# Attention: one unit in eight transposed on TensorE instead of by DMA

## The chip, the cores and the metric

One core of one Trainium2 chip runs the kernel. The metric is the device time of one execution in microseconds (us).

## The reference

Two layers of a backbone over 1024 latent tokens with 256 context tokens in front, width 1024. A layer projects the normed tokens once, into three parallel mixers (softmax attention, an mLSTM, a pooling mixer), joins them, projects them out, adds them to the stream, and applies a SwiGLU feed-forward. The change touches the attention alone:

```python
def one_block(qi):                      # 128 queries, 8 heads of 64, 2 key/value heads
    s = jnp.einsum('bqhgd,bkhd->bhgqk', qi, k, preferred_element_type=F32) * scale
    p = jax.nn.softmax(s, -1).astype(v.dtype)
    return jnp.einsum('bhgqk,bkhd->bqhgd', p, v)
```

Latent queries read all 1280 keys; context queries (layer 0 alone needs them) read the 256 context keys.

## The kernel before

Precision comes from pairs: an fp32 value is held as an f16 high part and an f16 remainder, and a product is three f16 matmuls (`TERMS`).

The attention stage of a layer begins at `phase("s")`. Its work is a list of units: one head of one tile of 128 latent queries (64 a layer), and in layer 0 also four units that hold four heads of a tile of context queries. Step i of the loop does these, in this order of the program:

- `front` of unit i: the scores, six matmuls into `Sp`, 128 x 1280 in PSUM (two such buffers); VectorE takes the row maximum `mx`; ScalarE writes the exponentials to `pf`, fp32 in SBUF (two buffers), with the row sums on the side.
- `split` of unit i-1: `pf` is cast to f16 (on ScalarE; on VectorE where the unit's index is divisible by 8) and GpSimd subtracts, which gives the pair `phl` (three buffers). One DMA transpose from SyncE's queue turns the pair into `pT` (five buffers), with the keys on the partitions.
- a fill: now and then one product of the output projection (`wout`, 12 f16 matmuls into `pwo`, which VectorE adds into the residual X). `pace` gives each step a budget, and a product of n columns costs n / 200 of it. Its weights are loaded by SyncE's queue (`st`) and split by ScalarE and VectorE (`hl`).
- `back` of unit i-5: 30 matmuls with `pT` as weights, into `pv`. After the eighth head `att_finish` scales the tile and turns it with another DMA transpose (`aoh`).
- one step of background threads (`pump`), the norms of finished token blocks among them.

In this stage PSUM holds two score buffers of three banks (`bank3`) and two single banks (`bank`). `pv` keeps one single bank for the eight heads of its tile; `pwo` and the norms take the other.

The Tile framework puts each engine's instructions in order by priority and readiness, close to the program's order, and places the semaphores; a buffer is reused when its last reader is done. Helpers record their operations at their own lines: L152 is `act` (ScalarE), L166 `stt` (VectorE), L169 `tt` (VectorE or GpSimd).

Of the kernel before, what the change touches and what calls it, by code (L numbers as in the profile page):

```python
# [10 lines left out]
F16 = mybir.dt.float16  # L11
# [7 lines left out]
P = 128  # L19
# [62 lines left out]
def hybrid_kernel(ctx: ExitStack, tc: tile.TileContext, I, out, dbg=None):  # L82
    nc = tc.nc
    V, S, G, TE, DMA = nc.vector, nc.scalar, nc.gpsimd, nc.tensor, nc.sync
    MUL, ADD, SUB, MAX, MIN = ALU.mult, ALU.add, ALU.subtract, ALU.max, ALU.min
# [10 lines left out]
    PFB, PHB, PTB = 2, 3, 5  # L96
# [21 lines left out]
    def bank(name="bk"):  # L118
        return cur["b"].tile([P, 512], F32, tag="bk", name=name)
# [8 lines left out]
    def pt_(shape, dt, tag, bufs=1, name=None):  # L128
        return cur["w"].tile(list(shape), dt, tag=tag, name=name or tag, bufs=bufs)
# [9 lines left out]
    def after(i, j):  # L139
        tc.add_manual_dep(i, j.name, order, reason="table order")  # L140

    def preload():

        p = S.preload_act_table_set("natural_log_exp_and_others").ins
        for j in tabs["last"]:
            after(p, j)
        tabs.update(pre=p, last=[], kind="el")

    def act(o, i, f=AF.Copy, **kw):
        if f in (AF.Exp, AF.Ln) and tabs["kind"] != "el":  # L150
            preload()
        b = S.activation(o, i, f, **kw).ins  # L152
        if f in (AF.Exp, AF.Ln):
            after(b, tabs["pre"])
            tabs["last"] = tabs["last"][-7:] + [b]
        elif f in (AF.Tanh, AF.Silu):
            if tabs["kind"] != f:
                for j in tabs["last"]:
                    after(b, j)
                tabs.update(last=[], kind=f)  # L160
            for j in tabs["last"][-1:]:
                after(b, j)
            tabs["last"] = [b]
# [4 lines left out]
    def tt(o, a, b, op, e=None):  # L168
        (e or V).tensor_tensor(o, a, b, op=op)  # L169
# [23 lines left out]
    def pump(n=1):  # L193
        for _ in range(n):
            for g in list(threads):
                try:
                    next(g)
                except StopIteration:
                    threads.remove(g)
# [18 lines left out]
    idn = con.tile([P, P], F32, name="idn")  # L218
# [305 lines left out]
    class Sums:  # L524


        def __init__(self, t0, n):
            self.t0, self.n, self.acc, self.k = t0, n, [], 0
# [212 lines left out]
    for l in range(DEPTH):  # L741
# [554 lines left out]

        class Unit:
            def __init__(self, i, qt, hs, qs):
                self.i, self.qt, self.hs, self.qs = i, qt, hs, qs
                self.nk, self.k0 = (NTOK, 0) if qt < 8 else (TC, T)  # L1300
                self.n = self.nk * len(hs)

# [25 lines left out]
                        accum_out=self.qs[1][:, h:h + 1])  # L1328

            def split(self):  # L1330
                i, n, pf = self.i, self.n, self.pf
                hl = pt_((P, 2, NTOK), F16, "phl", PHB)
                if i % 8 == 0:
                    V.tensor_copy(hl[:, 0, :n], pf[:, :n])
                else:
                    act(hl[:, 0, :n], pf[:, :n])
                tt(hl[:, 1, :n], pf[:, :n], hl[:, 0, :n], SUB, G)
                self.pT = pt_((P, 2, 10, P), F16, "pT", PTB)
                if n == NTOK:
                    DMA.dma_start_transpose(out=self.pT.rearrange("p a k c -> p (a k) c"), in_=hl.rearrange("p a t -> p (a t)"))  # L1340
                else:
                    for a in range(2):
                        DMA.dma_start_transpose(out=self.pT[:, a, :n // P], in_=hl[:, a, :n])

            def back(self):
                if self.hs[0] == 0:
                    self.qs[0] = bank("pv")
                nkt = self.nk // P
                for e, h in enumerate(self.hs):
                    kv = h // 4  # L1350
                    for kt in range(nkt):
                        for j, (a, b) in enumerate(TERMS):
                            mm(self.qs[0][:, h * 64:h * 64 + 64], self.pT[:, a, e * nkt + kt],
                               qkv[:, 6, b, self.k0 + kt * P:self.k0 + (kt + 1) * P][:, kv * 64:kv * 64 + 64],
                               start=(kt == 0 and j == 0), stop=(kt == nkt - 1 and j == 2))

        def att_finish(qt, pv_, sums):
            V.reciprocal(sums, sums)
            o = f2k((P, 8, 64), F32, "ao")
            tt(o, pv_.rearrange("p (h e) -> p h e", h=8), sums.unsqueeze(2).to_broadcast([P, 8, 64]), MUL)  # L1360
            oh = f2k((P, 4, 2, P), F16, "aoh")
            ov = o.rearrange("p (k x) e -> p k (x e)", x=2)
            act(oh[:, :, 0], ov)
            tt(oh[:, :, 1], ov, oh[:, :, 0], SUB)
            DMA.dma_start_transpose(out=mixT[:, 0:4, :, qt * P:(qt + 1) * P].rearrange("p k a t -> p (k a) t"),
                                    in_=oh.rearrange("p k a c -> p (k a c)"))
# [9 lines left out]
        def fills():  # L1376
            ctx_ = [] if last else [(T, TC)]
            sums = {}
            for key, k0, bl, qt in (("woa", 4, blks, -1), ("wob", 0, ctx_ + [(0, 512)], 3), ("woc", 0, [(512, 256)], 5)):
                if k0 == 0:  # L1380
                    for t0, n in bl:
                        sums[t0] = Sums(t0, n)
                for m in range(8):
                    while done[0] < qt:
                        yield 0
                    w = w_get((key, l, m))
                    for (t0, n) in bl:
                        if k0 == 0 and m:
                            sums[t0].step(G)
                        wout(w, k0, m, t0, n, bank("pwo")[:, :n])  # L1390
                        yield n / 200
                w = None
                if k0 == 0:
                    for t0, n in bl:
                        nt[t0] = chain(norm(l, 3, h2, t0, n, sums[t0].step(V)))
                        del sums[t0]
                if key == "wob":
                    dump(f"mix{l}", mixT)

        def first_ffn():  # L1400

            while now[0] < nu or any(g in threads for g in nt.values()):
                yield 0
            f0.update(wg=w_get(("gate", l, 0)), wu=w_get(("up", l, 0)), Sg=bank3("Sg"), Su=bank3("Su"))
            for t0, n in blks[2:] + [(0, 512)]:
                for w, S_ in ((f0["wg"], f0["Sg"]), (f0["wu"], f0["Su"])):
                    yield from fm_steps(S_[:, t0:t0 + n], w, h2, t0, n)
# [10 lines left out]
        units = []  # L1418
        for qt in range(8):
            qs = [None, pt_((P, 8), F32, "sums", 3)]  # L1420
            units += [Unit(len(units) + h, qt, [h], qs) for h in range(8)]
            if qt < 2 and not last:
                qs = [None, pt_((P, 8), F32, "sums", 3)]
# [2 lines left out]
        nt = {}  # L1426
        fill = fills()
        nu = len(units)
        budget = 0.0
        fill_ffn = first_ffn()  # L1430

        def pace(part):

            return (1.1 if part < 0.9 else 2.5) if last else 0.8 if part < 0.2 else 1.5

        for i in range(nu + 5):
            now[0] = i
            if i < nu:
                units[i].front()
            if 1 <= i <= nu:  # L1440
                units[i - 1].split()
            if i >= 3:
                budget = min(budget + pace(i / nu), 3.0)
                if budget > 0:
                    c = next(fill, None)
                    if c is None:
                        c = next(fill_ffn, 0)
                    budget -= c
            if i >= 5:
                u = units[i - 5]  # L1450
                u.back()
                if u.hs[-1] == 7:
                    att_finish(u.qt, *u.qs)
                    if u.qt < 8:
                        done[0] = u.qt
                units[i - 5] = u = None
            pump()
        for _ in fill:
            pass
        units = fill = None  # L1460
# [544 lines left out]
```

## Time and profile before

| | |
|---|---|
| median of three runs | 2797.26 us (2795.92 to 2797.89) |
| the profiled execution | 2801.78 us, span 2800.0 us, mean granted TensorE clock 0.967 |
| busy over the span | TensorE 92%, VectorE 67%, ScalarE 50%, GpSimd 46% |
| attention of layer 0 | scores from 372.6 us, transposes of the pairs from 383.1 us to about 668 |
| attention of layer 1 | scores from 1826.1 us, transposes from 1834.4 us to 2101.1 |

The profile is one execution on the chip. Times in it count from the start of its span. PE is TensorE's matmuls and PEld its weight loads, DVE is VectorE, ACT ScalarE, POOL GpSimd; SPq is SyncE, which issues the DMAs. L12 is line 12 of the kernel.

### The profile page before, as it was taken

The numbers are of one execution on the slowest core, as the hardware profiler recorded it, in microseconds if no ns is written. First come the engines' busy times: TensorE is split into PE (matmuls) and PEld (weight loads), VectorE is DVE, ScalarE is ACT, GpSimd is POOL, SyncE is SP. The second block draws the span as 40 slices with busy tenths as digits, with TensorE's granted clock in tenths as the row PEclk, the third lists the DMA queues.
The fourth block names the chain that finished last, engine by engine and source line by source line (L and its number), as shares of the span: only waits on it lengthen the run. The fifth ranks groups of instructions, "written<-read, shape, count | busy, mean of one in ns | idle before, by whom it ended". The sixth has DMA issues, their size and how long they took to land. (4 is left out here: it accounts for less than half of the span.)

```text
span 2800.0 us, 53595 instructions
## 1 busy us (share of the span) xinstructions
PE 2562.9 (92%) x21331; PEld 1496.8 (53%) x21331; DVE 1883.6 (67%) x3217; ACT 1387.2 (50%) x2650; POOL 1288.5 (46%) x979
## 2 busy tenths in 40 slices
PE   7999988887799999999999998988878799999997
PEld 5875555555455555555555674545554344444444
DVE  5458867779856655656566557866677766576666
ACT  5345457776443434434344445466764444444353
POOL 1124446674434434344443213456764555555651
PEclk9999999999899999999999999999999999999999
DMA  9544499996222232322212222499993121211211
GB/s 298 143 122 115 126 208 187 195 186 129 61 83 84 83 88 80 89 84 83 68 39 78 69 61 64 124 183 188 195 188 80 45 61 53 61 53 53 61 53 76
DMA packets 650640, 300.95 MB, mean 107 GB/s; under 512 B 381896, under 2 KB 639764, under 8 KB 649876
## 3 DMA queue, kind: packets, MB, share of 16 engines
q1 hardware_dynamic: 650212, 297.45, 44.2%
q8 instruction: 167, 2.74, 0.4%
q14 instruction: 85, 0.70, 0.1%
q10 hardware_dynamic: 176, 0.07, 0.0%
HBM read 176.19 MB, written 20.87 MB: 70 GB/s over the span
## 5 line engine op out<-in xcount | busy, mean ns | idle before, releaser
L1900 PEld LDWEIGHTS <-hlp 128*128 128x128 f16 x5040 | 492.9, 98 | 610.1 <-issue 49.5
L1900 PE MATMUL Swb<-T,hlp 128*128 128x512 f16 x1920 | 446.4, 382 | 30.8 <-DVE sg L166 14.7
L169 POOL TENSOR_TENSOR phl<-pf,phl 128x1280 f16<-128x1280 f32 (+1 forms) x132 | 346.3, 2625 | 187.7 <-ACT phl L152 129.4
L166 DVE SCALAR_TENSOR_TENSOR hlp<-ws,hlp 128x512 f16<-128x512 f32 (+1 forms) x320 | 228.9, 722 | 150.6 <-ACT hlp L152 119.9
L152 ACT ACTIVATE hlp<-ws 128x512 f16<-128x512 f32 (+1 forms) x320 | 163.6, 518 | 220.1 <-PE Swb L1900 89.8
L152 ACT ACTIVATE pf<-Sp,mx,rq 128x1280 f32<-128x1280 f32 (+1 forms) x144 | 189.2, 1315 | 103.4 <-DVE mx L1320 89.1
L1315 DVE TENSOR_REDUCE mx<-Sp 128x1 f32<-128x1280 f32 (+1 forms) x132 | 194.9, 1477 | 64.5 <-PE Sp L1311 59.5
L1371 PE MATMUL pwo<-T,hl 128*128 128x512 f16 (+1 forms) x960 | 196.5, 356 | 38.0 <-DVE X L166 20.0
L1900 PE MATMUL Swc<-T,hlp 128*128 128x512 f16 x960 | 227.2, 379 | 0.0
L1311 PE MATMUL Sp<-T 128*128 128x512 f16 (+1 forms) x800 | 172.9, 355 | 58.5 <-ACT pf L152 56.1
L1900 PE MATMUL Swb<-tq,hlp 128*128 128x512 f16 x960 | 220.5, 379 | 2.5 <-ACT T L152 2.3
L466 PE MATMUL pfm<-T,hl 128*128 128x512 f16 (+1 forms) x1032 | 217.0, 364 | 4.2 <-ACT E L152 4.1
L152 ACT ACTIVATE T<-sg 128x512 f16<-128x512 f32 (+1 forms) x170 | 100.0, 600 | 229.4 <-POOL sg L169 154.8
L166 DVE SCALAR_TENSOR_TENSOR hlp<-st,hlp 128x256 f16<-128x256 f32 (+1 forms) x201 | 141.6, 709 | 89.8 <-ACT hlp L152 75.1
L169 POOL TENSOR_TENSOR ws<-st 128x256 f32<-128x256 f32 (+1 forms) x97 | 102.2, 1061 | 185.6 <-DMA st<-in_w_ffn_down_dram 83.3
L1912 PE MATMUL dx<-T,hlp 128*128 128x256 f16 x1440 | 177.9, 273 | 10.6 <-DVE hlp L166 6.4
L169 POOL TENSOR_TENSOR X<-X,T 128x512 f32<-128x512 f32 x80 | 113.2, 1415 | 147.4 <-DVE X L166 111.1
L1900 PE MATMUL Swa<-T,hlp 128*128 128x512 f16 x720 | 169.1, 380 | 0.0
L1912 PEld LDWEIGHTS <-hlp 128*128 128x128 f16 x1440 | 139.3, 100 | 43.0 <-issue 9.1
L1371 PEld LDWEIGHTS <-hl 128*128 128x128 f16 x960 | 98.0, 103 | 119.8 <-issue 53.3
L152 ACT ACTIVATE phl<-pf 128x1280 f16<-128x1280 f32 (+1 forms) x115 | 144.9, 1261 | 30.3 <-DMA pT<-phl 27.9
L152 ACT ACTIVATE hlp<-st 128x256 f16<-128x256 f32 (+1 forms) x201 | 101.2, 510 | 114.6 <-PE Swb L1900 73.2
(320 smaller groups left out, 4733.6 us busy)
## 6 DMA issues: line engine op xcount, KB each, us to landing
T<-in_w_ada_dram SPq DMA_DIRECT2D x48, 512.0 KB
rawa<-in_w_ada_dram SPq DMA_DIRECT2D x48, 512.0 KB
st<-in_w_in_dram SPq DMA_DIRECT2D x32, 512.0 KB
st<-in_w_out_dram SPq DMA_DIRECT2D x64, 256.0 KB
st<-in_w_ffn_gate_dram SPq DMA_DIRECT2D x32, 512.0 KB
st<-in_w_ffn_up_dram SPq DMA_DIRECT2D x30, 512.0 KB
st<-in_w_ffn_down_dram SPq DMA_DIRECT2D x30, 512.0 KB
xs<-X SPq DMA_DIRECT2D x4, 2048.0 KB
```

Source lines behind the costliest of these rows:

```text
L152: b = S.activation(o, i, f, **kw).ins
L166: V.scalar_tensor_tensor(o, a, s, b, op0=o0, op1=o1)
L169: (e or V).tensor_tensor(o, a, b, op=op)
L466: mm(o, w[:, a, k, :], h[:, k, b, t0:t0 + n], start=(k == 0 and j == 0), stop=(k == nk - 1 and j == 2))
L1311: mm(Sp[:, e * nk + b0:e * nk + b0 + m], ql, qkv[:, 4 + h // 4, a, k0 + b0:k0 + b0 + m], start=(a == 0), stop=(a == 1), skip_group_check=True)
L1315: r = V.tensor_reduce(mx[:, :ne], Sp[:, :n].rearrange("p (e k) -> p e k", e=ne), axis=AX.X, op=MAX)
L1371: mm(pb, w[:, a, k, :], mixT[:, k0 + k, b, t0:t0 + n], start=(k == 0 and j == 0), stop=(k == 3 and j == 2))
L1900: mm(o, w[:, a, k, :], B[:, b], start=(s in "172" and k == 0 and j == 0), stop=(k == kh(i) - 1 and j == 2), skip_group_check=True)
L1912: mm(dbank[i][:, r * 256:(r + 1) * 256], w[:, a, k, :], B[:, b], start=(first and k == 0 and j == 0), stop=(not first and k == kh(i) - 1 a ...
```

## The change

Every eighth of the single-head units, from the sixth on, is turned on TensorE: 16 units in all. Such a unit has no `phl`, no DMA transpose and no GpSimd subtraction. Its `pf` is transposed in ten fp32 blocks of 128 x 128, four, four and two to a part. Each part takes one bank, `turn`; ScalarE copies the bank to the high half of `pT`, and VectorE writes the remainder. The three parts are placed in the step of the unit's `split`: before the fill, after the fill, and after `back`.

```diff
             def split(self):
                 i, n, pf = self.i, self.n, self.pf
+                if i in turned:
+                    self.pT = pt_((P, 2, 10, P), F16, "pT", PTB)
+                    self.parts = [self.turn(k, min(4, 10 - k)) for k in range(0, 10, 4)]
+                    return
                 hl = pt_((P, 2, NTOK), F16, "phl", PHB)
...
+            def turn(self, k, m):
+                def go():
+                    tb = bank("turn")
+                    for c in range(m):
+                        TE.transpose(tb[:, c * P:(c + 1) * P], self.pf[:, (k + c) * P:(k + c + 1) * P], idn)
+                    tv = tb[:, :m * P].rearrange("p (k c) -> p k c", k=m)
+                    act(self.pT[:, 0, k:k + m], tv)
+                    tt(self.pT[:, 1, k:k + m], tv, self.pT[:, 0, k:k + m], SUB)
+                return go
...
+        turned = [u.i for u in units if len(u.hs) == 1][5::8]
...
             if 1 <= i <= nu:
                 units[i - 1].split()
+                parts = units[i - 1].parts
+            if parts:
+                parts.pop(0)()
             if i >= 3:
                 budget = min(budget + pace(i / nu), 3.0)
...
+            if parts:
+                parts.pop(0)()
             if i >= 5:
                 u = units[i - 5]
                 u.back()
...
+            while parts:
+                parts.pop(0)()
             pump()
```

## Rows read from the trace of the kernel before

**Rows 1.** The page: busy us by engine, DMA share in 40 slices.

```profile
PE 2562.9 (92%) x21331; PEld 1496.8 (53%) x21331; DVE 1883.6 (67%) x3217; ACT 1387.2 (50%) x2650; POOL 1288.5 (46%) x979
...
DMA  9544499996222232322212222499993121211211
```

**Rows 2.** Stretches: length; busy us of PE, PEld, DVE, ACT, POOL; clock; DMA share; GB/s.

```profile
383.00:605.00 222.00, 195.31 (x2354) 125.62 (x2354) 160.22 (x192) 158.77 (x216) 153.48 (x65) 0.95 1.09 194
605.00:668.00 63.00, 48.68 (x634) 36.29 (x633) 55.97 (x68) 43.26 (x67) 40.61 (x23) 0.92 0.97 184
1840.00:2080.00 240.00, 194.51 (x2353) 122.22 (x2352) 163.90 (x194) 169.61 (x212) 164.07 (x66) 0.94 1.05 190
2080.00:2105.00 25.00, 18.80 (x308) 15.34 (x306) 22.77 (x27) 17.89 (x28) 15.57 (x10) 0.89 0.91 170
```

**Rows 3.** DMA view, 1840 to 2080 us: DMAs issued, with their count.

```profile
st<-in_w_out_dram SPq DMA_DIRECT2D x18, 256.0 KB
pT<-phl SPq DMA_TRANSPOSE x60
```

**Rows 4.** Timeline of SyncE, 1944 to 1981 us: start, us, issue, count.

```profile
1949.84 13.44 SPq L1340 DMA_TRANSPOSE pT<-phl  x4
...
1964.07 10.85 SPq L1340 DMA_TRANSPOSE pT<-phl  x3
1974.98 1.30 SPq L1365 DMA_TRANSPOSE T<-aoh  x1
```

**Rows 5.** Waits, 1847 to 2058 us: who for whom, us, times, longest.

```profile
ACT pf L152 <- DVE mx L1320: 34.6, 16, 6.1
...
ACT phl L152 <- DMA pT<-phl: 16.1, 11, 3.2
...
DVE phl L1334 <- DMA pT<-phl: 8.0, 3, 3.9
...
POOL phl L169 <- DMA pT<-phl: 3.7, 1, 3.7
```

**Rows 6.** Timeline of ScalarE, 1944 to 1955 us: first and last of four exponentials.

```profile
1944.04 1.42 ACT L152 ACTIVATE pf<-Sp,mx,rq 128x1280 f32<-128x1280 f32 x1 [3.01 <-DVE mx L1320]
...
1952.38 1.42 ACT L152 ACTIVATE pf<-Sp,mx,rq 128x1280 f32<-128x1280 f32 x1
```

**Rows 7.** Timeline of TensorE, 1938 to 1960 us: scores, then a fill.

```profile
1951.18 1.24 PE L1311 MATMUL Sp<-T 128*128 128x512 f16 x6
1952.26 2.75 PE L1371 MATMUL pwo<-T,hl 128*128 128x512 f16 x12
```

**Rows 8.** Groups by line and form, 1840 to 2080 us: busy, mean ns, idle before.

```profile
L169 POOL TENSOR_TENSOR phl<-pf,phl 128x1280 f16<-128x1280 f32 x59 | 155.1, 2629 | 71.8 <-ACT phl L152 55.5 <-DVE phl L1334 9.7 <-DMA pT<-phl 3.7
L1315 DVE TENSOR_REDUCE mx<-Sp 128x1 f32<-128x1280 f32 x59 | 87.6, 1484 | 27.9 <-PE Sp L1311 24.3 <-ACT phl L152 3.5
...
L152 ACT ACTIVATE phl<-pf 128x1280 f16<-128x1280 f32 x52 | 65.8, 1267 | 16.9 <-DMA pT<-phl 16.1
...
L166 DVE SCALAR_TENSOR_TENSOR X<-pwo,prm,X 128x512 f32<-128x512 f32 x23 | 17.2, 746 | 8.2 <-PE pwo L1371 8.2
```

**Rows 9.** Groups by line and form, 383 to 605 us.

```profile
L169 POOL TENSOR_TENSOR phl<-pf,phl 128x1280 f16<-128x1280 f32 x52 | 137.4, 2643 | 61.9 <-ACT phl L152 51.7 <-DVE phl L1334 7.4 <-POOL phl L169 1.2
```

**Rows 10.** Timeline of TensorE, 5 to 60 us: eight fp32 transposes each.

```profile
23.17 1.95 PE L233 MATMUL px<-idn,T 128*128 128x128 f32 x8
...
50.23 1.04 PE L233 MATMUL px<-idn,T 128*128 128x128 f32 x8
```

**Rows 11.** Instructions on `ptm`, a PSUM bank: count, ns min/median/max.

```profile
L152 ACT ACTIVATE T<-ptm x6: 383/578/597, 366.3 to 1825.2; 128x512 f16<-128x512 f32 x4, 128x256 f16<-128x256 f32 x2
L166 DVE SCALAR_TENSOR_TENSOR T<-ptm,T x6: 425/684/692, 367.4 to 1825.6; 128x512 f16<-128x512 f32 x4, 128x256 f16<-128x256 f32 x2
```

**Rows 12.** Stretches of the start, columns as in rows 2.

```profile
20.00:30.00 10.00, 5.99 (x57) 4.10 (x57) 4.92 (x8) 3.38 (x7) 0.00 (x0) 0.50 1.09 343
...
50.00:57.00 7.00, 6.77 (x71) 4.57 (x69) 4.80 (x10) 5.52 (x14) 2.21 (x2) 1.00 1.08 368
```

More of the change, by code (lines that the diff above doesn't have):

```diff
@@ L1298, in __init__ @@
             def __init__(self, i, qt, hs, qs):
-                self.i, self.qt, self.hs, self.qs = i, qt, hs, qs
+                self.i, self.qt, self.hs, self.qs, self.parts = i, qt, hs, qs, []
                 self.nk, self.k0 = (NTOK, 0) if qt < 8 else (TC, T)
@@ L1439, in hybrid_kernel @@
                 units[i].front()
+            parts = []
             if 1 <= i <= nu:
                 units[i - 1].split()
+                parts = units[i - 1].parts
+            if parts:
+                parts.pop(0)()
             if i >= 3:
```

## The prediction

> **What bounds the kernel now.** I read the page first, for where the time is spent: its slices show two stretches in which the DMA engines are at nine tenths or more, slices 6 to 9 and 26 to 29 [rows 1]. They are the two attention stages. The reader is to see there that TensorE, at 92% over the span, is not what stands out in them; the DMA engines are.
>
> Next, the view by stretches for those stages [rows 2]. In 383 to 605 us and 1840 to 2080 us the DMA share is 1.09 and 1.05 (packets overlap, so it passes 1), while TensorE is busy 195 of 222 and 195 of 240 us, ScalarE 159 and 170, VectorE 160 and 164, GpSimd 153 and 164. In the tails, 605 to 668 and 2080 to 2105, VectorE leads with 56.0 of 63 and 22.8 of 25.
>
> The DMA view counts 60 transposes `pT<-phl` in the 240 us [rows 3], so a unit takes 4.00 us. SyncE's own timeline says why: four transposes in 13.44 us and three in 10.85, with nothing between [rows 4], 24.3 / 7 = 3.47 us each. Eight units cost the queue 8 x 3.47 = 27.8, plus one transpose of `aoh`, 1.3, plus the `w_out` loads (18 in 60 units, so 2.4, at the 0.79 us between the end of the four transposes and the next three) 1.9: 31.0 of the 32.0 us that eight units take. So the queue is 97% occupied, and the waits show its pressure going back: ScalarE 16.1, VectorE 8.0 and GpSimd 3.7 us until a `phl` buffer was free [rows 5]. The larger wait for the row maximum, 34.6, follows from it in part, since VectorE is blocked behind its own cast. When nothing holds it, ScalarE starts four exponentials in a row between 1944.04 and 1952.38, 2.78 us apart [rows 6]. The front end can run faster than 4.00.
>
> The stretch moves 190 GB/s while the DMA engines never rest [rows 2]. The Trainium skill (Advanced Engine Details and Errata, X-Bar Transpose) expects 350 to 400 GB/s of a transposing DMA; as an estimate from that page, a unit's 128 x 2560 x 2 bytes would take 1.9 us at 350, the queue would stand half empty, and relieving it would be worth nothing. The trace disagrees with 3.47 us, and the measurement decides.
>
> **The change part by part.** It concerns 16 units of 132, eight in a layer: 5, 15, 25, 33, 41, 49, 57, 65 in layer 0 and 5, 13, ..., 61 in layer 1.
>
> *Removed*, per turned unit: one DMA transpose, 3.47 us of the queue; one GpSimd subtraction, 2.63; one ScalarE cast, 1.27 [rows 8] (none of the 16 has an index divisible by 8, where VectorE casts).
>
> *Added*: ten fp32 transposes of 128 x 128. The start of the program has the same instruction: eight take 1.04 us [rows 10], so 0.13 each and, with what the last of a group takes to end, about 0.6 for four and 0.38 for two, 1.6 for a unit. ScalarE copies out of PSUM to f16: 0.60 for 512 columns, 0.38 for 256 [rows 11], 1.58 in all, against 1.27 removed. VectorE subtracts out of PSUM: 0.68 and 0.42, 1.8 us in all, all of it new.
>
> *Eight units after*, layer 1: the queue 31.0 - 3.5 = 27.5; TensorE 194.5 / 60 x 8 = 25.9, plus 1.6 = 27.5. Both floors stand at 27.5, so the slack against 32.0 is 4.5. In layer 0's stretch GpSimd has 52 long units [rows 9] and the four context units, 56 in 222 us, 31.7 for eight; TensorE 195.3 / 56 x 8 = 27.9, plus 1.6 = 29.5, is the floor there: slack 2.2. ScalarE's 0.3 more and VectorE's 1.8 cost nothing in these stretches, where both are idle for a quarter of the time or more; in the tails VectorE's is priced. GpSimd's 2.63 less gains nothing by itself, as it is idle for a third.
>
> *The new wait.* One of the two banks of `bank()` is held by `pv` through a q tile, so the three parts and the fills (`pwo`) take turns in the other. And `pf` has two buffers: the exponential two units later waits until the last transpose has read it. Before, `pf` is free 1.27 + 2.63, with hand-overs some 4.1 us after its exponential. After, bare: 0.6 + 0.60 + 0.68, twice, plus 0.38: 4.2. Behind each of the two copies and subtractions that come first something can stand: half an exponential (0.7) on ScalarE and half a maximum (0.75) on VectorE, 2.9 for two. So `pf` is held h = 0.1 to 3.0 us longer. If a fill comes in between as well, its 2.75 [rows 7] and 0.75 for the add into X [rows 8] make it 6.5. I take 1.6: halfway between the first two, because TensorE starts a fill right behind the scores, at 1952.26 after the scores of 1951.18 [rows 7], while an exponential starts at 1952.38 [rows 6]; such a fill is ahead of the transposes, not between them. What queues behind a late `pf` is the exponential two units on, and behind that its scores buffer.
>
> *The sum.* Layer 1, seven units in the stretch: -(4.5 - 1.6) x 7 = -20.3. Layer 0, six: -(2.2 - 1.6) x 6 = -3.6. Three units (57 and 65, and 61 of layer 1) fall into the tails, where no queue is relieved: hold 1.6 plus VectorE's 1.8 at 90% occupation, 1.6: 3 x 3.2 = +9.6. Together -14.3; as a function of the hold, 16 h - 39.9. The profiled execution took 2801.8 us (span 2800.0); it would take 2787.5. It stands 4.5 above the median of the runs, 2797.3; the same step down from the median gives 2783. With h = 0.1 layer 1 gains no more than the queue's 3.5: -24.5 - 12.6 + 5.1 = -32, or 2765.
>
> **The rivals.** *The single bank decides (slower).* A fill gets between the first and the second part. The budgets of `pace` (0.8 a step, then 1.5, in layer 0, 1.1 in layer 1, against 2.56 for 512 columns), followed through the loop, put a fill into the very step of 11 of the 16 units: eight of 512 columns (3.5 us of bank each, as above) and three of 256 (about half, 1.9). That adds 8 x 3.5 + 3 x 1.9 = 33.7, and -14.3 becomes +19: 2817. It decides as soon as the mean hold passes 39.9 / 16 = 2.5 us. For it: the program puts the fill between the two parts. Against it: a fill's inputs are ready earlier than the transposes'. The Trainium skill speaks on this side (Perfetto Trace Analysis, Optimizing Tensor Performance): independent groups should rotate through different banks, so that evacuating one overlaps the next. No stretch shown here has transposes in one bank; what the rule would do here is this rival.
>
> *The queue is not the bound (no change).* SyncE would issue the transposes earlier and another loop keep the 4.00 us. For it: direct waits on the DMA are only 16.1 + 8.0 + 3.7 = 27.8 of 211 us, and a chain of waits among the three engines could set the same pace. Against it: the 97%. Time: 2797, give or take 5. The DMA rule above would lead here, and the row leaves it little.
>
> *TensorE's clock falls (slower).* Waits for the bank are gaps on TensorE. Eight transposes took 1.95 us where the granted clock was 0.50, 1.04 at 1.00 [rows 10, 12]; the stages stand at 0.94 and 0.95, the last tail at 0.89 [rows 2]. If both stages fell to 0.89, TensorE's eight units would take 25.9 x 0.94 / 0.89 + 1.6 = 29.0 and 27.9 x 0.95 / 0.89 + 1.6 = 31.4, the slacks would be 3.0 and 0.3, and the sum -(3.0 - 1.6) x 7 + (1.6 - 0.3) x 6 + 9.6 = +7.6: 2805.
>
> **How the numbers follow.** What a measurement can tell from no change is 0.2%, 5.6 us: h below 2.1 is faster, above 2.9 slower. The forecast, 2783 with 2765 to 2791 of its own, gets 0.47; no change 0.19; the bank 0.30; the clock 0.04. So faster 0.47, same 0.19, slower 0.34. The range, 2764 to 2816, takes in the bare hold and nearly all of the bank's price; it leaves out the full price of a fill between the parts of every unit that has one.
>
> **What would show it.** In the changed profile: 112 long transposes `pT<-phl`, 160 fp32 transposes into `turn`, GpSimd 116 subtractions; layer 1's stage about 17 us shorter (-20.3 + 3.2) and layer 0's some 3 longer (-3.6 + 6.4); the waits of ScalarE, VectorE and GpSimd for a `phl` buffer well below 27.8 in layer 1's stretch; SyncE idle for a few us after each turned unit. The step on the hold is wrong if the last transpose of a turned unit starts much more than 6 us after its exponential ends. The forecast is wrong if fills stand on TensorE between the parts of most units, or if VectorE's subtractions stand behind two maxima, not half of one.

## The result and the profile after

The changed kernel takes 2847.06 us (median of four runs, 2846.34 to 2848.71), the kernel before 2797.57 (four runs, 2795.92 to 2798.91): a ratio of 1.018, with a 95% interval of 1.016 to 1.020, so some 49.5 us slower. The prediction said 2783, at most 2816. The profiled execution has a span of 2845.7 us against 2800.0.

From the first scores to the last `pv`, layer 0's stage grew from 296.4 us (373.8 to 670.2) to 326.9 (375.0 to 701.9), layer 1's from 279.5 (1826.1 to 2105.6) to 291.7 (1857.0 to 2148.8). That is 30.5 + 12.3 of the 45.7 us between the spans.

The page after, busy time by engine and the DMA share in 40 slices, against [rows 1]:

```profile
PE 2591.2 (91%) x21491; PEld 1519.1 (53%) x21491; DVE 1910.4 (67%) x3265; ACT 1392.1 (49%) x2682; POOL 1238.3 (44%) x963
...
DMA  9544488876223222222212222488973111111211
```

Stretches after, columns as in [rows 2]: the body and the tail of layer 0's stage, the body of layer 1's.

```profile
383.00:630.00 247.00, 209.89 (x2428) 137.27 (x2427) 170.66 (x213) 160.79 (x228) 139.30 (x60) 0.94 0.85 159
630.00:690.00 60.00, 45.19 (x559) 32.79 (x560) 46.56 (x62) 38.54 (x62) 28.48 (x17) 0.89 0.74 143
1850.00:2110.00 260.00, 212.04 (x2512) 134.91 (x2510) 175.46 (x223) 169.65 (x220) 145.65 (x59) 0.95 0.86 163
```

The queue was relieved: the DMA share in the stages fell from 1.09 and 1.05 to 0.85 and 0.86. The time did not follow. No engine took its place: TensorE is busy 82% of layer 1's stretch (212.0 of 260), VectorE 67%, ScalarE 65%, where they stood at 81, 68 and 71% before. The clock stood at 0.95 and 0.94 before, at 0.94 and 0.95 after. So the stages are longer by waits. The waits after, 1879 to 2094 us (as [rows 5]: who for whom, us, times, longest):

```profile
POOL phl L169 <- ACT phl L152: 56.6, 21, 5.7
...
ACT pf L152 <- POOL phl L169: 21.2, 11, 2.8
PEld L1368 <- DMA pT<-phl: 21.1, 10, 3.4
PE pv L1368 <- DMA pT<-phl: 18.8, 10, 3.3
...
DVE X L166 <- PE pwo L1386: 10.0, 12, 2.0
...
ACT pT L152 <- PE turn L1354: 8.0, 6, 5.6
...
PE turn L1354 <- ACT pf L152: 4.9, 4, 2.5
...
ACT phl L152 <- DMA pT<-phl: 4.7, 4, 2.7
```

Two of these rows in the view before, 1847 to 2058 us:

```profile
POOL phl L169 <- ACT phl L152: 46.6, 33, 3.7
...
ACT pf L152 <- POOL phl L169: 0.5, 1, 0.5
```

The wait that the change was to shorten shrank: ScalarE for a free `phl`, 16.1 to 4.7; the rows of VectorE and GpSimd for one are gone. In its place the exponential waits for the subtraction that frees `pf` (0.5 to 21.2), GpSimd waits longer for the casts (46.6 to 56.6), and `pv` waits for DMA transposes that are issued late behind them. The queue is no longer full; it is fed late.

The matmuls, copies and subtractions on `turn` over the execution, and what TensorE, ScalarE and VectorE waited for ahead of them:

```profile
L1354 PE MATMUL turn<-idn,pf x160: 272/273/476, 400.5 to 2132.9; 128*128 128x128 f32 x160
L152 ACT ACTIVATE pT<-turn x48: 372/586/599, 402.8 to 2135.9; 128x512 f16<-128x512 f32 x32, 128x256 f16<-128x256 f32 x16
L169 DVE TENSOR_TENSOR pT<-turn,pT x48: 407/680/693, 403.7 to 2136.8; 128x512 f16<-128x512 f32 x32, 128x256 f16<-128x256 f32 x16
its engine sat idle before it (us, times) until:
  ACT pf L152: 44.4, 20
  PE turn L1354: 20.1, 17
  ACT pT L152: 14.6, 13
  DVE pT L169: 11.5, 17
```

The durations of the copies and subtractions are those of [rows 11]; four transposes take 0.66 us in the median, though six of the 32 groups take 1.1. The waits are the news: 44.4 us for an exponential (21.3 of TensorE's matmuls and 23.1 of its weight loads, which wait side by side), 20.1 of ScalarE for transposes.

One turned unit of layer 1 (index 13) shows how. TensorE, then ScalarE, VectorE and GpSimd (start, us, instruction, count, idle before it and what ended that):

```profile
1916.09 1.11 PE L1354 MATMUL turn<-idn,pf 128*128 128x128 f32 x4
...
1921.32 2.76 PE L1386 MATMUL pwo<-T,hl 128*128 128x512 f16 x12 [0.20 <-DVE pT L169]
...
1925.76 0.66 PE L1354 MATMUL turn<-idn,pf 128*128 128x128 f32 x4 [0.48 <-DVE X L166]
...
1930.10 0.44 PE L1354 MATMUL turn<-idn,pf 128*128 128x128 f32 x2 [2.40 <-DVE pT L169]
```

```profile
1914.54 1.40 ACT L152 ACTIVATE pf<-Sp,mx,rq 128x1280 f32<-128x1280 f32 x1
...
1917.42 1.42 ACT L152 ACTIVATE pf<-Sp,mx,rq 128x1280 f32<-128x1280 f32 x1 [1.38 <-POOL phl L169]
...
1918.83 0.59 ACT L152 ACTIVATE pT<-turn 128x512 f16<-128x512 f32 x1
...
1923.35 1.42 ACT L152 ACTIVATE pf<-Sp,mx,rq 128x1280 f32<-128x1280 f32 x1 [2.77 <-POOL phl L169]
...
1928.93 1.42 ACT L152 ACTIVATE pf<-Sp,mx,rq 128x1280 f32<-128x1280 f32 x1 [1.77 <-POOL phl L169]
```

```profile
1919.17 1.49 DVE L1315 TENSOR_REDUCE mx<-Sp 128x1 f32<-128x1280 f32 x1 [5.40 <-PE Sp L1311]
1920.58 0.68 DVE L169 TENSOR_TENSOR pT<-turn,pT 128x512 f16<-128x512 f32 x1
...
1926.71 2.74 DVE L166 SCALAR_TENSOR_TENSOR hl<-st,hl 128x512 f16<-128x512 f32 x1 [1.00 <-ACT hl L152]
1929.37 0.68 DVE L169 TENSOR_TENSOR pT<-turn,pT 128x512 f16<-128x512 f32 x1
```

```profile
1926.29 2.61 POOL L169 TENSOR_TENSOR phl<-pf,phl 128x1280 f16<-128x1280 f32 x1 [2.98 <-DVE X L166]
```

The first part starts at 1916.09, right behind its exponential. Its copy comes behind the next exponential, its subtraction behind a row maximum; then the fill takes the bank (1921.32), and the second part starts at 1925.76. Its subtraction stands behind a weight split that takes 2.74 us, and TensorE stands 2.40 us for it. The last part ends at 1930.54, so `pf` is held 14.6 us. Meanwhile one `pf` buffer is left, and the exponentials come 5.9 and 5.6 us apart instead of 2.78 [rows 6]. Over the sixteen units, from the exponential's end to the last transpose's, the mean is 10.6 us (5.9 to 16.1). Before, the same sixteen units held `pf` 4.7 us on the mean (exponential's end to subtraction's end), so the hold grew by 5.9. A fill stands between the first and second part in 11.

### The profile page after: what moved, and what is told of

It is laid out like the page before. It is cut to its first block, busy times and chain, and to the rows that moved or that the text cites. A ratio compares the mean times of both kernels' runs of the same rounds, so it can differ in the third digit from the quotient of the medians.

```text
span 2845.7 us, 53938 instructions
## 1 busy us (share of the span) xinstructions
PE 2591.2 (91%) x21491; PEld 1519.1 (53%) x21491; DVE 1910.4 (67%) x3265; ACT 1392.1 (49%) x2682; POOL 1238.3 (44%) x963
## 5 line engine op out<-in xcount | busy, mean ns | idle before, releaser
L1924 PE MATMUL Swb<-T,hlp 128*128 128x512 f16 x1920 | 444.6, 381 | 30.1 <-ACT T L152 27.3
L169 POOL TENSOR_TENSOR phl<-pf,phl 128x1280 f16<-128x1280 f32 (+1 forms) x116 | 303.3, 2618 | 267.5 <-ACT phl L152 155.2
L1386 PE MATMUL pwo<-T,hl 128*128 128x512 f16 (+1 forms) x960 | 191.2, 350 | 26.1 <-DVE X L166 12.2
L1311 PE MATMUL Sp<-T 128*128 128x512 f16 (+1 forms) x800 | 181.7, 362 | 24.8 <-ACT pf L152 22.5
L1368 PE MATMUL pv<-T,pT 128*128 128x64 f16 x3936 | 150.0, 196 | 32.1 <-DMA pT<-phl 24.7
L1368 PEld LDWEIGHTS <-pT 128*128 128x128 f16 x3936 | 143.3, 100 | 55.4 <-DMA pT<-phl 28.2
```

Source lines behind the costliest of these rows:

```text
L1311: mm(Sp[:, e * nk + b0:e * nk + b0 + m], ql, qkv[:, 4 + h // 4, a, k0 + b0:k0 + b0 + m], start=(a == 0), stop=(a == 1), skip_group_check=True)
L1386: mm(pb, w[:, a, k, :], mixT[:, k0 + k, b, t0:t0 + n], start=(k == 0 and j == 0), stop=(k == 3 and j == 2))
L1924: mm(o, w[:, a, k, :], B[:, b], start=(s in "172" and k == 0 and j == 0), stop=(k == kh(i) - 1 and j == 2), skip_group_check=True)
```

## The experiments

Each was run beside the kernel before on the same chip (2801.2 to 2802.3 us there). Differences are of medians; brackets hold the ratio's 95% interval. "Own buffer" means that a turned unit's exponentials go to `spare`, SBUF that is free in this stage, so that both `pf` buffers stay with the others.

**e1, own buffer; e2, all parts ahead of the fill; e3, both.**

```diff
-                self.pf = pt_((P, NTOK), F32, "pf", PFB)
+                self.pf = spare if self.i in turned else pt_((P, NTOK), F32, "pf", PFB)
```
```diff
-            if parts:
+            while parts:
                 parts.pop(0)()
             if i >= 3:
```

> The changed kernel, but a turned unit writes its exponentials to a place of its own, so that the two buffers of pf serve the other units alone. Theory H (the loss comes from pf, which a turned unit holds 10.6 us after its exponential on the mean, against some 4 before): the loss of 49 us goes, 2780 to 2805 us. Theory B (the loss comes from TensorE, which stands before parts and fills until the one free bank is emptied): nothing but the place has changed, 2835 to 2850.

> The changed kernel, but all three parts stand ahead of the fill of their step. H: the hold falls by the fill's 3.5 us and more, to 5 to 7 us, and most of the loss goes: 2795 to 2820. B: the bank has the same users and only their order differs; fills now wait for three parts: 2835 to 2855.

> Both edits together. H: as the first alone, since a pf of its own makes the order of the parts indifferent, within 8 us of it. B: as the second alone.

Measured: e1 +32.7 us [1.011, 1.014], e2 +52.2 [1.017, 1.020], e3 +42.1 [1.014, 1.017]. So the hold of `pf` is worth 17 us (49.5 - 32.7), not nearly all. e2 takes every fill out from between the parts and shortens the mean hold to 8.5 us, and gains nothing: the three parts then stand on TensorE one behind the other, each until the bank is cleared (its rows ahead of `turn`: DVE pT 18.9 against 11.5 in the change, PE turn 32.1 against 20.1). e3 lies between the two, as neither theory said.

**e4, relief only.** The sixteen units take a constant for their weights: no transposition of theirs at all, no cast, no subtraction, and their `pv` waits for nothing.

```diff
-                    self.pT = pt_((P, 2, 10, P), F16, "pT", PTB)
-                    self.parts = [self.turn(k, min(4, 10 - k)) for k in range(0, 10, 4)]
+                    self.pT = fixed
```

> Leaves out the turning of the 16 units: their weights are a constant, so neither DMA nor TensorE turns anything, and cast and subtraction go too. It shows what the relief of the queue is worth with no price. If the queue set the pace, 13 units at 2 to 3.5 us: 2750 to 2775. If it did not: 2790 to 2800.

Measured: -26.5 us [0.989, 0.992]; layer 0's stage 285.8 us (-10.6), layer 1's 262.4 (-17.0). That is what all the relief is worth together, so what was put in its place costs 76. It isn't the queue's alone: GpSimd's subtraction (2.63 us) and ScalarE's cast (1.27) go with the DMA transpose. e16 below puts work of 1.6 us back on ScalarE and loses nothing by the medians, so the cast is hardly it; no run parts the queue from GpSimd.

**e5, own buffer and the parts one step later; e6, own buffer and one part a step, in the steps u+2 to u+4, behind `back`.**

```diff
                 units[i - 1].split()
-                parts = units[i - 1].parts
+            if 2 <= i <= nu + 1:
+                parts = units[i - 2].parts
```

> The turned unit keeps its own exponential buffer, and its three parts are issued one step later than in e1, so that no transpose stands on TensorE ahead of its exponential. Theory 'order' (TensorE runs its instructions in a fixed order; the first transpose stands in front of pv products and scores until its exponential has ended, about 24 us over both stages, and what is behind it is late): at least 15 us under e1's +33, that is +5 to +18 us against the kernel before, and the waits of turn for an exponential under 5 us. Theory 'bank' (copies and subtractions must clear the one single bank that fills and parts share): +25 to +40, as e1. Theory 'work' (the copies and subtractions cost ScalarE and VectorE their time wherever they stand): +25 to +35.

> As e5, but one part a step, in the three steps that follow the one after the unit's exponential, each behind the step's pv products. Theory 'order': as e5 or better, 0 to +15 us against the kernel before. Theory 'bank': better than e1, since a part has a whole step for its bank, +10 to +20, but with the waits of turn and pwo for the bank gone. Theory 'work': +25 to +35, as e1.

Measured: e5 +9.1 us [1.002, 1.004], e6 +2.0 [1.000, 1.002]. Only the place differs from e1, and most of the 32.7 us is gone. The waits of `turn` for an exponential are gone too. Both keep waits for the bank (rows ahead of `turn`: DVE pT 25.7 and DVE X 9.9 in e5, DVE X 24.8 and DVE pT 9.1 in e6).

**e7, no transposes; e8, no copies**, both with the own buffer and the places of e1.

```diff
-                    tb = bank("turn")
...
-                    tv = tb[:, :m * P].rearrange("p (k c) -> p k c", k=m)
+                    tv = self.pf[:, k * P:(k + m) * P].rearrange("p (k c) -> p k c", k=m)
```

> Leaves out the 160 transposes and the bank: the unit keeps its own exponential buffer, ScalarE copies the same three pieces of it straight into the halves of the weights and VectorE subtracts, so that the sixteen units' weights are not turned. Theory 'work': +15 to +35 us against the kernel before, near e1's +33. Theories 'order' and 'bank': -25 to -10, near e4's -26, since neither TensorE nor a bank takes part.

> Leaves out the copies and subtractions: the unit keeps its own exponential buffer and is transposed on TensorE into the bank as in e1, but nothing reads the bank, and the sixteen units' pv products take other values for weights. Theory 'order': the stall of the first transpose stays, 0 to +20 us against the kernel before. Theory 'bank': -25 to -10, since a part frees its bank as soon as it has ended. Theory 'work': -25 to -10 as well.

Measured: e7 -8.1 us [0.995, 0.998], between the theories; e8 +5.0 [1.001, 1.003]. With nothing reading the bank, the transposes alone take back the relief and more.

**e11, one transpose in place of ten; e12, the same one step later.** Nothing else of the turn is left in them.

```diff
-                    self.parts = [self.turn(k, min(4, 10 - k)) for k in range(0, 10, 4)]
+                    self.parts = [self.turn(0, 1)]
```

> e8 with one transpose instead of ten in each of the sixteen units, at the place of the first part; copies, subtractions and the other nine transposes are left out, and the sixteen units' pv products take other values for weights. The one transpose costs TensorE 0.3 us at most. Theory 'order' (it is the place in front of pv products and scores that costs, by the wait for the exponential): -5 to +10 us against the kernel before, 15 us or more above e4's -26. If e8's +31 over e4 was the transposes' own time: -26 to -20.

> e11 with the one transpose placed one step later. Theory 'order': -26 to -18 us against the kernel before, 15 us or more under e11. Otherwise as e11.

Measured: e11 -2.5 us [0.998, 1.000], e12 -23.3 [0.991, 0.994]. Instructions on `turn` and the waits ahead of them (matmuls and weight loads together), e11 and then e12:

```profile
L1354 PE MATMUL turn<-idn,T x16: 272/328/477, 399.8 to 2080.0; 128*128 128x128 f32 x16
its engine sat idle before it (us, times) until:
  ACT T L152: 54.4, 23
```

```profile
L1354 PE MATMUL turn<-idn,T x16: 272/273/421, 399.4 to 2069.0; 128*128 128x128 f32 x16
its engine sat idle before it (us, times) until:
  DVE X L166: 10.6, 6
```

Sixteen transposes, 16 x 0.3 = 5 us of work, cost 21 us by their place alone: behind the scores of the next unit and ahead of other products, waiting for an exponential that is not done. TensorE's matmuls alone stand 26.0 us for it in e11, in 11 waits; one step later no such wait is left. One of them, on TensorE in e11 (`T` in the second line is the unit's own buffer):

```profile
1941.38 0.55 PE L1365 MATMUL pv<-T,pT 128*128 128x64 f16 x13 [0.34 <-DMA pT<-phl]
1945.62 0.48 PE L1354 MATMUL turn<-idn,T 128*128 128x128 f32 x1 [3.69 <-ACT T L152]
1945.89 0.63 PE L1311 MATMUL Sp<-T 128*128 128x512 f16 x1
1946.32 3.77 PE L1383 MATMUL pwo<-T,hl 128*128 128x512 f16 x12
...
1950.80 0.66 PE L1365 MATMUL pv<-T,pT 128*128 128x64 f16 x17
```

One transpose stands 3.69 us in the middle of a unit's `pv` products, of which 13 are done. Scores, a whole fill and the other 17, which read the same `pT`, follow it, none with a wait of its own. The 21 us are good to about 5: the two profiled executions differ by 17.2, of which 12.8 lie in the two stages.

**e13, e7 with the copies and subtractions one step later; e16, e7 without the subtractions** (the low halves are other values). e13's edit is that of e5; e16 leaves out the `tt` of `turn`.

> e7 (no transposes on TensorE, no bank; ScalarE copies and VectorE subtracts straight from the unit's own exponential buffer, so that the sixteen units' weights are not turned) with the three parts one step later. Theory 'order' (copies and subtractions stand on ScalarE and VectorE in front of other units' work until their input is there): -26 to -18 us against the kernel before, 10 us or more under e7's -8. Theory 'work' (the 1.6 and 1.8 us of the engines are worth what they take, wherever they stand): -12 to -3, as e7.

> e7 without the subtractions: in the sixteen units ScalarE copies the exponentials straight to the weights' high halves in three pieces, the low halves are other values, and there are no transposes and no bank. If ScalarE's copies cost nothing in their place (the engine is idle for a quarter of the time): -28 to -22 us against the kernel before, as e4, and e7's 18 us were the subtractions' and their meeting with GpSimd. If the copies cost their 1.58 us a unit: about -10, as e7.

Measured: e13 +8.8 us [1.002, 1.005], which both theories missed; e16 -26.1 [0.990, 0.993], as e4. So the work of ScalarE's copies costs nothing that the medians show, to within some 6 us (their waits for transposes are not in e16), and e7's 18 us come with the subtractions. VectorE's subtractions in e13:

```profile
L169 DVE TENSOR_TENSOR pT<-T,pT x48: 409/678/2741, 404.0 to 2098.5; 128x512 f16<-128x512 f32 x32, 128x256 f16<-128x256 f32 x16
```

Read from SBUF, some are four times as long as the 0.69 us that none of the 48 passes from PSUM in the change: 13 are over 1 us in e13, 3 in e7 (counted in the instructions' own times), and all 48 take 43.8 us together against 32.6. So VectorE works 11 us more in e13; whether that is what makes it 17 us slower than e7 is not shown. Neither run prices the change's own subtractions.

**e14, e1 with copies and subtractions that read the exponentials in SBUF**, so that the same transposes stand in the same places but a bank is free once they end.

```diff
-                    tv = tb[:, :m * P].rearrange("p (k c) -> p k c", k=m)
+                    tv = self.pf[:, k * P:(k + m) * P].rearrange("p (k c) -> p k c", k=m)
```

> e1 with the copies and subtractions reading the exponentials in SBUF instead of the bank: the same transposes, copies and subtractions in the same places, but nothing reads the bank, and the sixteen units' weights are not turned. Theory 'chain through the bank': +15 to +24 us against the kernel before, 9 us or more under e1's +33. If the parts simply do not add up (the same waits counted otherwise): +28 to +35, as e1.

Measured: +13.2 us [1.004, 1.007], 19.5 under e1, a little below the range of the chain's theory. That is the chain through the single bank: a part, its copy, its subtraction, a fill, its add, the next part. The edit undoes two of its links at once, the copy's wait for the transposes and the bank's wait for copy and subtraction. e14's subtractions are longer than e1's (37.1 us against 28.5 in all), so the chain is not overrated by them. The adds of the fills in layer 0's stage, 374 to 700 us, e1 and then e14 (busy, mean ns, idle before):

```profile
L166 DVE SCALAR_TENSOR_TENSOR X<-pwo,prm,X 128x512 f32<-128x512 f32 x24 | 18.0, 749 | 39.1 <-PE pwo L1386 39.1
```

```profile
L166 DVE SCALAR_TENSOR_TENSOR X<-pwo,prm,X 128x512 f32<-128x512 f32 x24 | 17.9, 746 | 16.9 <-PE pwo L1386 16.9
```

VectorE stands less than half as long for fills once they need not wait for the parts' bank. The gain is in this stage: layer 0's takes 307.0 us in e14 against 321.3 in e1. Layer 1's takes 281.7 against 281.9, though the same wait falls there from 16.6 to 8.8; in layer 1 the chain cost nothing that these executions show.

**e9, e6 in layer 1 alone; e10, e9 with no fill in the four steps of a turned unit; e15 and e17, every fourth unit of layer 1** (in e15 the third part reads what the next turned unit has written to the shared buffer; in e17 it comes a step earlier).

```diff
-        turned = [u.i for u in units if len(u.hs) == 1][5::8]
+        turned = [u.i for u in units if len(u.hs) == 1][5::8] if last else []
```
```diff
-                if budget > 0:
+                if budget > 0 and not due:
```

> e6 with layer 1's eight units alone turned; layer 0 is as before. In e6 layer 1's stage took 273.4 us against 279.5 and layer 0's 308.6 against 296.4. Theory 'slack' (what the queue's relief is worth is bounded by the engine next in line, and in layer 0 that engine leaves less): -6 to -12 us against the kernel before, with layer 1's stage near 273. If the two stages of e6 had merely traded time at their border: within 3 us of the kernel before.

> e9, and in the four steps between the turned unit's exponential and its last part no fill is issued (the budget may save up to 6 instead of 3 in layer 1, and the fills follow in the other four steps), so that parts and fills no longer share the bank. Theory 'bank still costs' (about 10 us of e6 over both layers): 3 to 8 us under e9. If the waits for the bank are covered: within 3 us of e9, or above it by what the fills left to the end of the stage cost.

> e9 with every fourth unit of layer 1 turned instead of every eighth: 15 units, none in layer 0. If the queue's relief still pays after e9's eight units: -14 to -20 us against the kernel before. If the next limit is reached (TensorE, ScalarE and the bank): 0 to +15.

> e15 with the third part issued together with the second, a step before the next turned unit's exponential writes the shared buffer; every fourth unit of layer 1 turned, none of layer 0. If e15's +5 came from that buffer: -20 to -10 us against the kernel before, below e9's -10. If the next limit is reached (TensorE, ScalarE and the bank): -5 to +8.

Measured: e9 -10.4 us [0.995, 0.998], 2791.96: faster than both kernels. Where it gains is not shown. Its profiled execution has layer 1's stage at 276.2 us, not near the 273 of theory 'slack', and layer 0's, where nothing is turned, at 292.9 against 296.4; so a stage varies by some 3 us between executions. Of the 14.8 us between the two spans 8 lie outside both stages, and the mean granted clock of e9's five runs is 0.970 against 0.966 in those of the kernel before beside it, so the clock may have a share in the 10.4. e10 is +14.4 [1.004, 1.007]: layer 1's stage took 286.8 us. It doesn't show the bank's price, since it also moves the fills; what of it costs so much stays open. e15 is +5.2 [1.001, 1.003] and e17 +16.1 [1.005, 1.008], with layer 1's stage at 286.7 and 294.1 us: twice the dose costs more than it relieves, and e17 more than either of its theories allowed.

## Why the prediction was wrong

Put in order, the runs make a ladder (us against the kernel before; in the last column the lengths of the two stages in the profiled executions, summed, against 575.9):

| run | what is in it | us | the rung | stages |
|---|---|---|---|---|
| e4 | relief alone | -26.5 | | -27.7 |
| e12 | one transpose, a step later, with its own buffer | -23.3 | +3 | -15.8 |
| e11 | it stands where the first part stands | -2.5 | +21 | -3.0 |
| e8 | all ten, nothing reads the bank | +5.0 | +7.5 | +8.0 |
| e14 | copies and subtractions, not from the bank; `pv` waits for them | +13.2 | +8 | +12.8 |
| e1 | from the bank | +32.7 | +19.5 | +27.3 |
| the change | with a shared `pf` | +49.5 | +17 | +42.7 |

The intervals of the runs are +-3 to +-5 us wide, so a rung is good to 4 to 7. The rungs of 21, 19.5 and 17 are clear of that, and the stages show all three (13, 14.5 and 15); the rung of 3 is not, and those of 7.5 and 8 hardly. A rung also depends on what is there already, and Tile plans the neighbours' order anew for each kernel: copies and subtractions cost 18 put on e4 (e7) and 8 put on e8.

*What bounds the kernel*: right in kind, as far as e4 goes: the relief pays (the page's second stretch is slices 27 to 30, a slip of one). Its size was not right: the slacks of 4.5 and 2.2 us per eight units add up to 31.5 + 13.2 = 44.7 us; measured 26.5, 10.6 in layer 0 and 17.0 in layer 1. Layer 0's 13.2 was near; layer 1's 31.5 was taken as if its stage would run down to the floors. The queue was also less full than 97%: the 3.47 us come from seven transposes in a row, while the 60 of layer 1's stretch take 3.37 on the mean, and SyncE's issues fill 91% of that stretch (94% of layer 0's). In e4 they fill 86% in the bodies of both stages (383 to 605 and 1832 to 2060 us), so neither floor was reached; what holds e4's stages there is not shown.

*The costs of the single instructions*: right. Four transposes take 0.66 us, copies 0.59, subtractions 0.68 and 0.41, and "ScalarE's 0.3 more costs nothing" held for the work itself (e16). VectorE's 1.8 us was priced at nothing in the stretches too. What it costs stays open: subtractions that read SBUF, some of them of the slower kind, cost 18 us in e7 (against e16) and, with the copies, 8 from e8 to e14.

*The new wait: this step failed.* "I take 1.6 ... such a fill is ahead of the transposes, not between them." The mean hold grew by 5.9 us, and a fill was between the first two parts in as many units, 11, as the budgets gave. The argument went by readiness, and the order on TensorE decided: the fill had been put behind the first part, and in e11 scores and a fill with no wait of their own stand behind a transpose that waits 3.69 us. The same argument hid the largest single rung. TensorE was priced by 1.6 us of work and by no wait; its first transpose, placed where its input is not done, costs 21 us over sixteen units (e11 against e12).

*The sum* then let the whole price hang on one variable, 16 h - 39.9. With the measured 5.9 it gives +54.5, close to +49.5, but by luck: the hold is worth 17 us, not 16 x 5.9 = 94, and the sum has no term for TensorE's wait (21) or the chain through the bank (19.5).

*The rivals.* "The single bank decides" named the sign and a true mechanism, and its condition, a mean hold above 2.5, was met. It priced fills between parts at 33.7 us; e2 shows that taking them away gains nothing by itself, since the parts then wait for each other in the same bank. What the bank costs is the chain, 19.5 us (e1 against e14), so it is not the whole of the loss. The Trainium skill's rule on rotating banks (Perfetto Trace Analysis, Optimizing Tensor Performance) points the right way here. "The queue is not the bound" fell with e4, as far as that run can tell the queue from GpSimd. "The clock falls" fell with the stretches after: 0.94 and 0.95 in the bodies of the stages against 0.95 and 0.94 [rows 2]; only layer 0's tail is lower, 0.89 against 0.92.

*What would show it*: the counts came as said (the page's instruction numbers, 160 transposes), and the waits for `phl` fell as said; layer 1's stage was 12 us longer instead of 17 shorter, layer 0's 30 longer instead of 3. Both named signs of being wrong came too: the hold far over 6 us, and fills between the parts of most units.

## What to carry to other kernels

An instruction is priced by its duration and by what stands behind it on its engine while its input is not ready: here 5 us of transposes cost some 21 by standing one step too early, and e12 got that back by moving them. Before work is moved between engines, write down the order on the engine that receives it and, for each shared buffer (here one PSUM bank and one of two `pf`), the chain that must end before the next user; idle shares say nothing of either. The relief of the queue (with GpSimd's) was worth six tenths (26.5 of 44.7 us) of what the floors promised. Of the kernels that do the whole work, only e9, spread out and in layer 1 alone, came out faster than the kernel before, for reasons not shown.

## What the runs showed of the hardware

VectorE's subtraction with two operands in SBUF and GpSimd's subtraction hold each other up. In e7, VectorE and then GpSimd:

```profile
2002.82 3.44 DVE L169 TENSOR_TENSOR pT<-T,pT 128x512 f16<-128x512 f32 x2
```

```profile
2003.15 2.82 POOL L169 TENSOR_TENSOR phl<-pf,phl 128x1280 f16<-128x1280 f32 x1 [4.73 <-ACT phl L152]
```

The first of VectorE's two began ahead of GpSimd's and took its usual 0.68 us, and GpSimd's took 2.82 instead of 2.63; the second began inside it and ended 0.3 us behind its end, after 2.84. It is no single case. In e7, e13 and e14, 110 such subtractions of VectorE began outside any GpSimd instruction, and none took more than 0.70 us; 34 began inside one, and all but one of them took from 0.74 to 2.84. In the change, where one operand is in PSUM, 17 began inside one and none took more than 0.69. The Trainium skill says the same (SBUF — State Buffer, Who interferes with whom): a VectorE instruction with two SBUF inputs contends with a GpSimd instruction that reads SBUF, and one with at most one SBUF input, outside certain fast modes, does not. In the change itself the weight split of 2.74 us at 1926.71 (1.22 in the median), on which the second part waited, began 0.4 us behind the start of a GpSimd subtraction.
